# Values projected token-major, and their convolution by shifted reads of a scratch

## The chip, the cores and the metric

One core of a Trainium2 chip runs the whole layer. The metric is the device time of one execution in microseconds; the time of a kernel is the median of its runs. The engines are TensorE (PE, with its weight loads as PEld), VectorE (DVE), ScalarE (ACT), GpSimd (POOL) and SyncE (SP), which issues nearly all DMAs in order.

## The reference

A decoder layer with two parallel mixers over 256 tokens of width 2048, everything in float32. Cut to what matters here:

```python
h = rms_norm(x, norm_pre_w) * (1 + scale) + shift
proj = h @ w_in                                   # 24656 columns
qkv = causal_conv_silu(gdn_qkv, gdn_conv_w)       # 4 taps over tokens, each channel by itself
q_a, k_a, v_a = split(qkv)                        # 16 heads of q and k, 32 of v, 128 channels each
q_a, k_a = l2_normalize(q_a) * 128**-0.5, l2_normalize(k_a)   # each serves two value heads
o_a = gated_delta_rule(q_a, k_a, v_a, g_log, beta)            # a unit lower triangular solve
o_a = rms_norm(o_a, gdn_norm_w) * silu(gdn_z)
y_a = o_a @ w_proj_gdn
# mLSTM branch y_b (its own conv of q and k), then
out = (sigmoid(gate_a) * y_a + sigmoid(gate_b) * y_b) @ w_out
return x + gate * rms_norm(out, norm_post_w)

def causal_conv_silu(x, w):
    xp = pad(x, 3 tokens in front)
    return silu(sum(xp[:, j:j + s] * w[j] for j in range(4)))
```

## The kernel before

All large products run on TensorE as three matmuls for each float32 product. A weight piece (`raw`, 128x1024 of a 1 MB load) is split by ScalarE into a high part (`whi`, L173) and by VectorE into the rest (`wlo`, L177); `h` is held split as `h_hi` and `h_lo`.

`Stream` walks one list of weight pieces in order. It loads ahead into three 1 MB buffers, prepares (splits) up to four pieces ahead of use into four buffers of each part, emits the matmuls of a piece, and then calls `side.step()` once. Everything that is not a weight product is written as a generator in `Side`: at each step every generator runs to its next `yield`, so a `yield from wait(3)` means that three weight pieces go by. `side.debt` counts VectorE microseconds, 1.6 are forgiven a step, and `side.room` holds the triangular solve back while the debt is high. The whole order on each engine is fixed when the program is built; on the chip an engine waits in order for what it needs. A tile's next use in its ring of buffers waits for the readers of its last.

A weight group has 512 columns, and two forms of product:

- `add_proj_t` (`pt`, L639 and L643): channels on partitions, tokens on the free axis. The weights are the stationary operand; a 512-column matmul moves `h_hi` and `h_lo` together and a 256-column one moves `h_hi` against the low weights. The group goes in two halves of 256 columns, four pieces each.
- `add_proj_n` (`pn`, through `mm3`, L244): tokens on partitions. `h` is stationary and 512 weight columns move, three matmuls for each block of 128 tokens and of the depth. Eight pieces.

A GDN period `gdn_period(zg)` covers two head pairs, `2 * zg` and `2 * zg + 1`. A head pair is one group of 512 columns: q, k and two value heads. The stream has the first pair (8 pieces, `add_proj_t`), the z group (8, `add_proj_n`) and the second pair (8). There are eight periods, and then four mLSTM periods, the two output projections and the last product.

For a head pair `conv_half` does the convolution channel-major, where a token shift is a shift on the free axis: q and k as the first half, the two values as the second. It adds the two parts of the projection (L688), scales by the last tap (ScalarE, L691), adds the other three taps with six VectorE instructions (L697) and takes the silu (L705). `gdn_stage1` then splits q and k (L752), loads the decay rows (`gb`, L723), masks them on GpSimd (`dd`, L730), makes the products of k with k and q (`psa`, `psb`), transposes k (L766) and the two values (`psv`, L771), takes the exponentials (L738 to L740) and writes the scaled score matrices `au`. The values go out of `psv` scaled by the norm of k into `rr` (L812). `block_rows` writes diagonal blocks to a DRAM scratch `ud`, `base_inverse` reads them back as `ug` (L832) and solves on VectorE (L838 to L857), and `gdn_stage2`, 31 steps after the first stage, applies the inverse to `rr`.

`gates` runs once before, ahead of the GDN stage, and makes the decay rows. `late_c["gcv"]` holds the conv weights with channels on partitions.

Of the kernel before, what the change touches and what calls it, by code (L numbers as in the profile page):

```python
# [15 lines left out]
P = 128  # L16
# [102 lines left out]
def hybrid_layer_kernel(  # L119
# [41 lines left out]
    def load_w(src):  # L161
        raw = wp.tile([P, 2048], F32, name="raw", tag="raw", bufs=3)
        c = 0
        for s_ in src if isinstance(src, tuple) else (src,):
# [108 lines left out]
    gate_row_dr = dr.tile([1, D], F32, name="gate_row_dr")  # L273
    START = [40 + g for g in range(8)] + [33, 37, 34, 38, 35, 39]
# [260 lines left out]
    def gates(ps):  # L535
# [52 lines left out]
        SP.dma_start(rows[32:40], mm_[64:72])  # L588
        yield from wait(3)
# [6 lines left out]
        V.tensor_scalar(ngt, tt[:, :, 0:32], -1.0, None, op0=ALU.mult)  # L596

# [28 lines left out]
    def add_proj_t(g, first, after, extra=None):  # L626

        w = w_in[g].rearrange("p (k n) -> p k n", k=KC)
        st_ = {}
        for hf in range(2):  # L630
            for t in range(2):
# [20 lines left out]
                stream.add(w[:, t * 8:(t + 1) * 8, hf * S:(hf + 1) * S], prep_w, use, after=done if t else None)  # L652
# [3 lines left out]
    def add_proj_n(g, after, extra=None):  # L656

        st_ = {}
        for t in range(4):
            def use(h, hi, lo, t=t):  # L660
                if t == 0 and h == 0:
                    st_["ps"] = [jtile(f"pn{i}") for i in range(2)]
                for kc in range(2):
                    k = t * 4 + h * 2 + kc
                    o = kc * 512
                    for b in range(2):
                        mm3(st_["ps"][b], h_hi[:, k, b * P:(b + 1) * P], h_lo[:, k, b * P:(b + 1) * P],
                            hi[:, o:o + 512], lo[:, o:o + 512], k == 0, k == KC - 1)
            stream.add(w_in[g][:, t * 2048:(t + 1) * 2048], prep_w, use, after=
                       (lambda: after(st_["ps"])) if t == 3 else None)  # L670
            if extra:
                extra()

    def conv_half(ps, taps, dst, hf, add=1, late=0, home=0, whole=False):

        if home and hf == 0:
            pair = bp.tile([P, 2, S], F32, name="ab", tag="ys", bufs=1)
            ab = [pair[:, i] for i in range(2)]
        elif home:
            ab = [bp.tile([P, S], F32, name="ab", tag=t, bufs=1) for t in ("p2", "tmp")]  # L680
        else:
            ab = [yp.tile([P, S], F32, name="ab", tag=("ya", ("yhi", "ylo")[i])[hf], bufs=3 - hf) for i in range(2)]
# [23 lines left out]

    def gdn_qk(ps, taps, qs, r, late):

        yield from conv_half(ps, taps, qs, 0, 1, late)
        qh = bp.tile([P, 2, S], F32R, name="qh", tag="qh", bufs=1)  # L710
        A.copy(qh, qs[:, 0:2])
        r.update(qh=qh)
# [29 lines left out]
    def gdn_taps(p):  # L742
        return lambda n, j: late_c["gcv"][:, (p * 4 + n) * 4 + j:(p * 4 + n) * 4 + j + 1]

    def gdn_stage1(p, ps, qs, pr, res):
# [6 lines left out]
        V.tensor_tensor(ql, qs[:, 0:2], qh.bitcast(F32), op=ALU.subtract)  # L752
        yield
        gb = decay_rows(2 * p)
# [4 lines left out]
        yield from banks(3)  # L759
# [5 lines left out]
        for m in range(2):  # L765
            T.transpose(psb[:, 256 + m * P:256 + (m + 1) * P], qs[:, 0, m * P:(m + 1) * P], ident)  # L766
        psv = gtile("psv", True)
        side.debt -= 1.6
        for blk in range(2):
            for h in range(2):  # L770
                T.transpose(psv[:, (blk * 2 + h) * P:(blk * 2 + h + 1) * P],  # L771
                            qs[:, 2 + h, blk * P:(blk + 1) * P], ident)
# [6 lines left out]
        if z == 0:  # L779
            res["eq"] = bp.tile([P, 2, 2], F32, name="eq", tag="eq", bufs=3)  # L780
            res["rr"] = bp.tile([P, 2, 2, S], F32, name="rr", tag="rr")
# [13 lines left out]
        for blk, ps_, n, c0 in ((0, psa, 256, 0), (1, psb, 128, 512)):  # L795
# [8 lines left out]
            if blk == 0:  # L804
                sk = bp.tile([P, 2], F32, name="sk", tag="sk")
# [3 lines left out]
        block_rows(res, z)  # L809
        yield  # L810
        for blk in range(2):
            A.activation(res["rr"][:, blk, z], psv[:, blk * S:(blk + 1) * S], AF.Copy, scale=sk[:, blk:blk + 1])  # L812
        gfree(psv)
# [66 lines left out]
    def gdn_stage2(zg, res, zr):  # L880
# [71 lines left out]

        rr = res["rr"].rearrange("p b z (h d) -> p b (z h d)", h=2)
# [81 lines left out]
    def period_tail(zg, ps, qs, pr, res, zr):  # L1035
        yield from gdn_stage1(2 * zg + 1, ps, qs, pr, res)
# [14 lines left out]
    def gdn_period(zg):  # L1051
        res = {}

        def pair(z, after):
            p, pr = 2 * zg + z, {}
            add_proj_t(p, lambda ps, qs: gdn_qk(ps, gdn_taps(p), qs, pr, 2 if z else 5),
                       lambda ps, qs: side.add(after(ps, qs, pr)))
# [499 lines left out]
```

## Time and profile before

| | |
|---|---|
| median of 3 runs | 1570.53 us (1570.4 to 1570.74) |
| profiled execution, its own time | 1570.67 us |
| its span | 1568.9 us |
| granted TensorE clock, mean | 0.998 |
| GDN stage, one period | 79.0 us, 24 weight pieces |
| GDN stage in the trace | about 334 to 966 us |
| mLSTM stage | to about 1180 us |

The span is cut into stages by time; a window of 79 us inside the GDN stage holds one period's work of every kind, though of three different periods, since the solve and the second stage trail the projection. Busy time of matmuls counts overlapping ones more than once, so the time of a matmul in a stream is read from one start to the next. A row such as `L697 DVE ... x24 | 10.1, 477 | 0.0` gives line, engine, operation, tiles, shapes and count, then busy us, mean ns of one, and the idle time before them with what ended it.

### The profile page before, as it was taken

The page shows a single profiled execution, that of the slowest core. Times are in us where ns is not written, and L with a number is a line of the kernel's source. Part 1 is how long each engine was busy: PE and PEld are TensorE (multiplying, and loading weights), DVE is VectorE, ACT ScalarE, POOL GpSimd, SP SyncE. Part 2 cuts the span into 40 slices and gives each one's busy share as a digit, 9 for nine tenths or more (in the row PEclk, how much of TensorE's full clock was granted, in tenths as well). Part 3 has the DMA queues.
Part 4 walks back from the last instruction along what each step waited for, and adds up shares of the span by engine and source line. Part 5 has one row for each costly group of instructions (what it writes and reads, how often), then busy time and mean ns, then how long its engine had stood idle before and what let it go on. Part 6 is the DMA issues. An engine that isn't in the chain of part 4 may idle for free.

```text
span 1568.9 us, 23204 instructions
## 1 busy us (share of the span) xinstructions
PE 1555.8 (99%) x8574; PEld 1308.5 (83%) x8574; DVE 1166.0 (74%) x1901; ACT 967.5 (62%) x1629; POOL 261.5 (17%) x212
## 2 busy tenths in 40 slices
PE   8999999999999999999999999999999999999997
PEld 5888888888888888888888888888888888888886
DVE  6785556765789898989898988776868866756654
ACT  7754446765666676767676777766566554544443
POOL 5787771000000010101010101000000000100100
PEclk9999999999999999999999999999999999999999
DMA  9998775975565656565656565657779877766573
GB/s 379 403 387 328 274 282 196 287 251 194 171 209 174 194 166 201 172 200 173 200 173 200 173 200 179 194 166 250 274 271 343 312 268 290 287 237 243 211 268 108
DMA packets 167739, 372.22 MB, mean 237 GB/s; under 512 B 26021, under 2 KB 127797, under 8 KB 140105
## 3 DMA queue, kind: packets, MB, share of 16 engines
q1 hardware_dynamic: 167240, 370.13, 68.2%
q8 instruction: 67, 1.10, 0.3%
q10 hardware_dynamic: 290, 0.53, 0.1%
q14 instruction: 46, 0.38, 0.1%
q0 software_dynamic: 96, 0.09, 0.0%
HBM read 354.40 MB, written 16.31 MB: 236 GB/s over the span
## 4 chain that ended last, share of the span: by engine, by line
PE 83%; issue 13%; DMA 2%; POOL 1%; ACT 1%; DVE 0%; SPq 0%; DVEq 0%; POOLq 0%; ACTq 0%
PE pn L244 38%; PE pt L639 19%; PE pt L643 9%; PE py L244 8%; POOL mg L1347 1%; DMA raw<-in_dram 1%; PE psa L244 1%; PE csil L314 0%; PE po L989 0%; PE po L988 0%; PE pc L978 0%; PE pb L968 0%; PE pa L960 0%; PE po L986 0%; PE pt L1028 0%
## 5 line engine op out<-in xcount | busy, mean ns | idle before, releaser
L177 DVE TENSOR_TENSOR wlo<-raw,whi 128x1024 fp32r<-128x1024 f32 (+1 forms) x455 | 558.8, 1236 | 221.6 <-ACT whi L173 220.5
L173 ACT CAST whi<-raw 128x1024 fp32r<-128x1024 f32 x508 | 523.9, 1046 | 269.4 <-PE pn L244 138.0
L244 PE MATMUL pn<-whi,h 128*128 128x512 f32 x1792 | 563.8, 392 | 1.2 <-ACT part L488 0.5
L639 PE MATMUL pt<-h,whi 128*128 128x512 f32 x1280 | 407.9, 400 | 0.0
L244 PEld LDWEIGHTS pn<-whi,h 128*128 128x128 f32 x1792 | 336.3, 188 | 72.3 <-ACT h L173 1.1
L244 PE MATMUL pn<-wlo,h 128*128 128x512 f32 x896 | 348.8, 389 | 0.0
L643 PEld LDWEIGHTS pt<-h,wlo 128*128 128x128 f32 x1280 | 240.4, 188 | 56.6
L643 PE MATMUL pt<-h,wlo 128*128 128x256 f32 x1280 | 251.9, 278 | 0.0
L639 PEld LDWEIGHTS pt<-h,whi 128*128 128x128 f32 x1280 | 195.5, 189 | 1.9
L244 PEld LDWEIGHTS pn<-wlo,h 128*128 128x128 f32 x896 | 168.3, 188 | 33.6
L177 POOL TENSOR_TENSOR wlo<-raw,whi 128x1024 fp32r<-128x1024 f32 (+1 forms) x67 | 146.5, 2199 | 47.3 <-ACT whi L173 41.6
L244 PE MATMUL py<-whi,yhi 128*128 128x512 f32 x384 | 150.6, 392 | 0.0
L244 PE MATMUL py<-whi,ylo 128*128 128x512 f32 x384 | 149.6, 390 | 0.0
L244 PE MATMUL py<-wlo,yhi 128*128 128x512 f32 x384 | 149.4, 389 | 0.0
L173 ACT CAST yhi<-ya 128x512 fp32r<-128x512 f32 x48 | 29.9, 623 | 127.6 <-PE py L244 124.3
L486 DVE TENSOR_TENSOR part<-pn,part 128x512 f32<-128x512 f32 x112 | 73.8, 686 | 45.1 <-PE pn L244 44.9
L730 POOL TENSOR_SCALAR_AFFINE_SELECT dd<-gb 128x256 f32<-128x256 f32 x40 | 33.9, 870 | 435.4 <-DMA gb<-rows 398.9
L177 DVE TENSOR_TENSOR ylo<-ya,yhi 128x512 fp32r<-128x512 f32 x48 | 33.2, 691 | 75.3 <-ACT yhi L173 71.8
L244 PEld LDWEIGHTS py<-whi,yhi 128*128 128x128 f32 x384 | 72.1, 188 | 15.3
L244 PEld LDWEIGHTS py<-whi,ylo 128*128 128x128 f32 x384 | 72.1, 188 | 15.1
L244 PEld LDWEIGHTS py<-wlo,yhi 128*128 128x128 f32 x384 | 72.1, 188 | 14.9
L697 DVE SCALAR_TENSOR_TENSOR qs<-ab,gcv,qs 128x255 f32<-128x255 f32 (+2 forms) x192 | 81.0, 477 | 0.0
(264 smaller groups left out, 1602.8 us busy)
## 6 DMA issues: line engine op xcount, KB each, us to landing
raw<-in_dram SPq DMA_DIRECT2D x259, 1024.0 KB
ar<-in_dram SPq DMA_DIRECT2D x31, 1024.0 KB
raw<-in_dram SPq DMA_DIRECT2D x16, 512.0 KB
ya<-o_dr SPq DMA_DIRECT2D x32, 256.0 KB
gate_dr<-part SPq DMA_DIRECT2D x11, 512.0 KB
gb<-rows SPq DMA_DIRECT2D x20, 256.0 KB
raw<-in_dram SPq DMA_DIRECT2D x6, 768.0 KB
ug<-ud SPq DMA_DIRECT2D x32, 128.0 KB
```

Of the source, the lines that this page charges most:

```text
L173: A.copy(hi, src)
L177: eng.tensor_tensor(lo, src, hi.bitcast(F32), op=ALU.subtract)
L244: T.matmul(ps, l, r, start=start and i == 0, stop=stop and i == 2, skip_group_check=True)
L486: V.tensor_tensor(part[g][:, b], ps[b], part[g][:, b], op=ALU.add)
L639: T.matmul(ps, hi[:, o:o + P], h2[:, k].rearrange("p a s -> p (a s)"), start=k == 0, stop=k == KC - 1, skip_group_check=True)
L643: T.matmul(ps[:, 0:S], lo[:, o:o + P], h_hi[:, k], start=False, stop=k == KC - 1, skip_group_check=True)
L697: V.scalar_tensor_tensor(dst[:, n, sh:], ab[i][:, 0:S - sh], taps(n, 3 - sh), dst[:, n, sh:], op0=ALU.mult, op1=ALU.add)
L730: G.affine_select(dd[:, :, blk * S:blk * S + P], gb[:, :, blk * P:(blk + 1) * P], pattern=[[0, 2], [1, P]], compare_op=ALU.is_ge, fill=-1e ...
L1347: G.tensor_tensor(mcols(b, hf, cg), mcols(b, hf, cg), s_, op=ALU.add)
```

## The change

The q and k halves of both head pairs of a period now form one channel-major group (two halves of 256 columns, one for each pair, 8 pieces); the four value heads form one token-major group of 512 columns (`add_proj_n`, 8 pieces); z follows. The weight arrays stay as they are: the two groups are read as column halves of the two old ones, so a unit of value weights is loaded with two DMAs.

The values are copied out of PSUM into `rr`, tokens on partitions. A token shift is now a shift across partitions, so they are written to a DRAM scratch `vd` with three zero rows in front, and read back shifted by one, two and three tokens. The tap weights are needed along the free axis: they are transposed once in `gates`, written to a scratch `conv_dr`, and read broadcast to all partitions, `ws`, for each pair. For each pair GpSimd multiplies shifts 2 and 3 by their taps and adds them, VectorE does so for shifts 0 and 1, and VectorE adds the two sums. One silu covers all four heads, and four ScalarE instructions scale by the norm of k. The transposes `psv` and the separate `gdn_qk` are gone. `conv_half` keeps its q and k work, now inside `gdn_stage1`, with its temporary in the ring `ylo`.

```diff
     def load_w(src):
...
+        for i, s_ in enumerate(src if isinstance(src, tuple) else (src,)):
+            if isinstance(src, tuple) and len(s_.shape) == 3:
+                SP.dma_start(raw.rearrange("p (k g c) -> p k g c", k=4, g=2)[:, :, i], s_)
+                continue
...
+    conv_dr = dr.tile([NPAIR, 4, 4, P], F32, name="conv_dr")
+    vd = dr.tile([S + 3, 512], F32, name="vd")
...
 # in gates
+        for z in range(2):
+            SP.dma_start(vd[0:3, z * S:(z + 1) * S], zz[0:3])
...
+        G.tensor_copy(gcp.rearrange("c (p t n) -> c p t n", n=4, t=4),
+                      late_c["gcv"].rearrange("c (p n t) -> c p t n", n=4, t=4))
+        yield from wait(2)
+        tc_ = gtile("tc")
+        for b in range(2):
+            T.transpose(tc_[:, b * P:(b + 1) * P], gcp[:, b * P:(b + 1) * P], ident)
+        A.copy(gct, tc_[:, 0:S])
+        yield from wait(2)
+        for b in range(2):
+            SP.dma_start(conv_dr[8 * b:8 * b + 8].rearrange("p t n c -> (p t n) c"), gct[:, b * P:(b + 1) * P])
...
 # in gdn_stage1
-        yield from conv_half(ps, gdn_taps(p), qs, 1, *((1, 0) if z else (3, 1)))
-        qh = pr["qh"]
+        yield from conv_half(ps, gdn_taps(p // 2), qs, z)
+        qz = qs[:, 2 * z:2 * z + 2]
+        qh = bp.tile([P, 2, S], F32R, name="qh", tag="qh", bufs=1)
+        A.copy(qh, qz)
+        gb = decay_rows(2 * p)
+        yield from wait(1 + z)
...
-        yield from banks(3)
+        yield from banks(2)
...
-        psv = gtile("psv", True)
-        side.debt -= 1.6
-        for blk in range(2):
-            for h in range(2):
-                T.transpose(psv[:, (blk * 2 + h) * P:(blk * 2 + h + 1) * P],
-                            qs[:, 2 + h, blk * P:(blk + 1) * P], ident)
+        side.debt -= 1.2
...
-        for blk in range(2):
-            A.activation(res["rr"][:, blk, z], psv[:, blk * S:(blk + 1) * S], AF.Copy, scale=sk[:, blk:blk + 1])
-        gfree(psv)
+    def gdn_values(zg, ps, res):
+        rr = bp.tile([P, 2, 2, S], F32, name="rr", tag="rr")
+        for b in range(2):
+            A.copy(rr[:, b].rearrange("p z c -> p (z c)"), ps[b])
+        yield from wait(2)
+        SP.dma_start(vd[3:].rearrange("(b t) c -> t b c", b=2), rr.rearrange("p b z c -> p b (z c)"))
+        ws = [bp.tile([P, 4, S], F32, name="cw", tag="qs") for _ in range(2)]
+        def tap_rows(z):
+            SP.dma_start(ws[z], conv_dr[2 * zg + z, :, 2:4].rearrange("t n c -> t (n c)").unsqueeze(0)
+                         .broadcast_to([P, 4, S]))
+        def shifted(z, j):
+            v = yp.tile([P, 2, S], F32, name=f"v{j}", tag="yhi" if z and j > 1 else "ya", bufs=2 if z and j > 1 else 3)
+            SP.dma_start(v, vd[3 - j:3 - j + S, z * S:(z + 1) * S].rearrange("(b t) c -> t b c", b=2))
+            return v
+        def tap(e, z, v, j):
+            side.debt += 0.7 if e is V else 0.0
+            e.tensor_tensor(v, v, ws[z][:, 3 - j].unsqueeze(1).broadcast_to([P, 2, S]), op=ALU.mult)
+        def plus(e, a, b):
+            side.debt += 0.7 if e is V else 0.0
+            e.tensor_tensor(a, a, b, op=ALU.add)
+        tap_rows(0)
+        yield from wait(3)
+        vs = [[rr[:, :, z], None, None, None] for z in range(2)]
+        for z, j in ((0, 1), (0, 2), (0, 3), (1, 2), (1, 3)):
+            vs[z][j] = shifted(z, j)
+        tap_rows(1)
+        yield from wait(3)
+        for z in range(2):
+            v = vs[z]
+            tap(G, z, v[2], 2)
+            tap(G, z, v[3], 3)
+            plus(G, v[2], v[3])
+            tap(V, z, v[0], 0)
+            yield
+            tap(V, z, v[1], 1)
+            yield
+            plus(V, v[0], v[1])
+            if z == 0:
+                vs[1][1] = shifted(1, 1)
+            yield
+            plus(V, v[0], v[2])
+            yield
+        A.activation(rr, rr, AF.Silu)
+        yield
+        for z in range(2):
+            for b in range(2):
+                A.activation(rr[:, b, z], rr[:, b, z], AF.Copy, scale=res["sk", z][:, b:b + 1])
+        res["rr"] = rr
...
 # in gdn_period
-        pair(0, lambda ps, qs, pr: gdn_stage1(2 * zg, ps, qs, pr, res))
+        pair = 2 * zg, 2 * zg + 1
+        add_proj_t(pair, lambda ps, qs: gdn_stage1(pair[0], ps, qs, res),
+                   lambda ps, qs: side.add(period_tail(zg, ps, qs, res, zrs[zg])))
+        add_proj_n(pair, lambda ps: side.add(gdn_values(zg, ps, res)))
         add_z(zg)
-        pair(1, lambda ps, qs, pr: period_tail(zg, ps, qs, pr, res, zrs[zg]))
```

More of the change, by code (lines that the diff above doesn't have):

```diff
@@ L626, in add_proj_t @@
     def add_proj_t(g, first, after, extra=None):
-        w = w_in[g].rearrange("p (k n) -> p k n", k=KC)
         st_ = {}
         for hf in range(2):
+            w = w_in[g[hf] if isinstance(g, tuple) else g].rearrange("p (k n) -> p k n", k=KC)
+            c0 = 0 if isinstance(g, tuple) else hf * S
             for t in range(2):
@@ L651, in done @@
                         after(st_["ps"], st_["dst"])
-                stream.add(w[:, t * 8:(t + 1) * 8, hf * S:(hf + 1) * S], prep_w, use, after=done if t else None)
+                stream.add(w[:, t * 8:(t + 1) * 8, c0:c0 + S], prep_w, use, after=done if t else None)
                 if extra:
@@ L668, in use @@
                             hi[:, o:o + 512], lo[:, o:o + 512], k == 0, k == KC - 1)
-            stream.add(w_in[g][:, t * 2048:(t + 1) * 2048], prep_w, use, after=
+            if isinstance(g, tuple):
+                src = tuple(w_in[i].rearrange("p (k n) -> p k n", k=KC)[:, 4 * t:4 * t + 4, S:2 * S] for i in g)
+            else:
+                src = w_in[g][:, t * 2048:(t + 1) * 2048]
+            stream.add(src, prep_w, use, after=
                        (lambda: after(st_["ps"])) if t == 3 else None)
@@ L681, in conv_half @@
         else:
-            ab = [yp.tile([P, S], F32, name="ab", tag=("ya", ("yhi", "ylo")[i])[hf], bufs=3 - hf) for i in range(2)]
+            pair = yp.tile([P, 2, S], F32, name="ab", tag="ylo", bufs=2)
+            ab = [pair[:, i] for i in range(2)]
         for i in range(2):
@@ L705, in conv_half @@
         A.activation(dst[:, 2 * hf:2 * hf + 2], dst[:, 2 * hf:2 * hf + 2], AF.Silu)
[L707 to L712, printed above, removed]
     o_dr = dr.tile([32, P, S], F32, name="o_dr")
@@ L740, in decay_exp, with gdn_taps, taps, gdn_stage1 @@
             A.activation(dd[:, h, S:384], dd[:, h, S:384], AF.Exp, bias=b22[:, h:h + 1])
-    def gdn_taps(p):
-        return lambda n, j: late_c["gcv"][:, (p * 4 + n) * 4 + j:(p * 4 + n) * 4 + j + 1]
-    def gdn_stage1(p, ps, qs, pr, res):
-        z = p % 2
-        yield from conv_half(ps, gdn_taps(p), qs, 1, *((1, 0) if z else (3, 1)))
-        qh = pr["qh"]
+    def gdn_taps(zg):
+        def taps(n, j):
+            c = ((2 * zg + n // 2) * 4 + n % 2) * 4 + j
+            return late_c["gcv"][:, c:c + 1]
+        return taps
+    def gdn_stage1(p, ps, qs, res):
+        z = p % 2
+        yield from conv_half(ps, gdn_taps(p // 2), qs, z)
[4 more added lines that the diff above has]
+        yield from wait(1 + z)
         side.debt += 0.7
         ql = bp.tile([P, 2, S], F32R, name="ql", tag="ql", bufs=1)
-        V.tensor_tensor(ql, qs[:, 0:2], qh.bitcast(F32), op=ALU.subtract)
-        yield
-        gb = decay_rows(2 * p)
+        V.tensor_tensor(ql, qz, qh.bitcast(F32), op=ALU.subtract)
         dd = decay_mask(gb)
@@ L804, in gdn_stage1 @@
             if blk == 0:
-                sk = bp.tile([P, 2], F32, name="sk", tag="sk")
+                res["sk", z] = sk = bp.tile([P, 2], F32, name="sk", tag="sk", bufs=4)
                 pow_(sk, sse[:, 2:4], phalf[:, 0:2])
@@ L951, in gdn_stage2 @@
         yield
+        while "rr" not in res:
+            yield
         rr = res["rr"].rearrange("p b z (h d) -> p b (z h d)", h=2)
@@ L1033, in gdn_stage2, with period_tail @@
             SP.dma_start(o_dr[4 * zg + 2 * z:4 * zg + 2 * z + 2].rearrange("h d t -> d h t"), oT)
-    def period_tail(zg, ps, qs, pr, res, zr):
-        yield from gdn_stage1(2 * zg + 1, ps, qs, pr, res)
+    def period_tail(zg, ps, qs, res, zr):
+        yield from gdn_stage1(2 * zg + 1, ps, qs, res)
         yield
@@ L1052, in gdn_period @@
         res = {}
[L1054 to L1057, printed above, removed]
-        pair(0, lambda ps, qs, pr: gdn_stage1(2 * zg, ps, qs, pr, res))
+        pair = 2 * zg, 2 * zg + 1
+        add_proj_t(pair, lambda ps, qs: gdn_stage1(pair[0], ps, qs, res),
+                   lambda ps, qs: side.add(period_tail(zg, ps, qs, res, zrs[zg])))
+        add_proj_n(pair, lambda ps: side.add(gdn_values(zg, ps, res)))
         add_z(zg)
-        pair(1, lambda ps, qs, pr: period_tail(zg, ps, qs, pr, res, zrs[zg]))
     def mlstm_taps(m):
```

5 lines of the change are left out of this document (2 added, 3 removed).

## The prediction

> **What bounds the kernel now.** I read the busy table first, then the windows of single stages, then the chain that ended last and TensorE's own list of waits.
>
> ```profile
> span 1568.9 us, 23204 instructions
> PE 1555.8 (99%) x8574; PEld 1308.5 (83%) x8574; DVE 1166.0 (74%) x1901; ACT 967.5 (62%) x1629; POOL 261.5 (17%) x212
> ...
> PE 83%; issue 13%; DMA 2%; POOL 1%; ACT 1%; DVE 0%; SPq 0%; DVEq 0%; POOLq 0%; ACTq 0%
> ```
>
> ```profile
> core 0: us, PE busy (x) PEld busy (x) DVE busy (x) ACT busy (x) POOL busy (x), PEclk, DMA share, GB/s
> 0.00:334.00 334.00, 328.85 (x1443) 266.23 (x1444) 223.71 (x265) 202.67 (x267) 174.57 (x110) 1.00 0.84 313
> ...
> 571.00:650.00 79.00, 79.00 (x546) 68.33 (x545) 68.95 (x150) 56.77 (x115) 7.66 (x9) 1.00 0.59 185
> 650.00:729.00 79.00, 79.00 (x546) 68.33 (x546) 69.08 (x149) 56.77 (x115) 7.66 (x9) 1.00 0.60 185
> ```
>
> One 79 us window is one period of the GDN stage (two head pairs and a z group, 24 weight pieces, so 79 / 24 = 3.29 us a step). There are eight periods. In them TensorE is busy 79.00 of 79.00 us at full granted clock, VectorE 69.08, ScalarE 56.77. TensorE's waits in the whole program come to 5.3 us, none of them in this stage:
>
> ```profile
> PE csil L314 <- ACT ar L312: 4.0, 1, 4.0
> PE pn L244 <- ACT part L488: 0.5, 1, 0.5
> PE pn L244 <- DVE part L490: 0.5, 1, 0.5
> PE pn L244 <- ACT h L173: 0.3, 1, 0.3
> ```
>
> So the period lasts as long as TensorE's instruction list takes to issue. A change here is worth what it removes from that list, unless it makes a feeder late.
>
> **TensorE, the term that counts.** A busy row double-counts pipelined matmuls, so I take start-to-start times from the timeline:
>
> ```profile
> 640.20 0.63 PE L639 MATMUL pt<-h,whi 128*128 128x512 f32 x2
> 640.66 0.40 PE L643 MATMUL pt<-h,wlo 128*128 128x256 f32 x2
> ...
> 651.34 0.62 PE L639 MATMUL pt<-h,whi 128*128 128x512 f32 x2
> ...
> 653.31 0.60 PE L771 MATMUL psv<-con,qs 128*128 128x128 f32 x4
> 653.66 0.48 PE L244 MATMUL pn<-whi,h 128*128 128x512 f32 x1
> ...
> 656.29 0.61 PE L244 MATMUL pn<-whi,h 128*128 128x512 f32 x2
> ...
> 661.73 0.61 PE L244 MATMUL pn<-whi,h 128*128 128x512 f32 x2
> ```
>
> 1. Channel-major (pt): 16 rounds of two 512- and two 256-column matmuls from 640.20 to 651.34, 0.696 us each. Token-major (pn): 8 rounds of three 512-column matmuls from 656.29 to 661.73, 0.680 us. Both rounds stream 1536 columns and a piece has four, so a piece costs 2.785 against 2.72 us. The first pn rounds after an insertion are slower (653.66 to 656.29 is 2.63 us for 11 matmuls, 0.717 a round), 0.14 us over 11 x 0.227 and so about 0.02 on each of the group's eight pieces: an estimate of 2.74. The change turns 8 pieces a period, 64 in all, from pt to pn: 64 x 0.045 to 0.065 = 2.9 to 4.2 us. I take 3.5, the middle, since v's group will also have insertions in it.
> 2. The transposes psv of the values go, since the values arrive token-major: 653.31 to 653.66, 0.35 us for four, once in each of 16 first stages: 5.6 us.
> 3. Added: two transposes of the conv weights in the gate stage, at under 0.1 us each by the psv row, plus the switch of shape: 0.3 us.
>
> Sum: 1570.67 (profiled execution: span 1568.9 and 1.8 around it) - 3.5 - 5.6 + 0.3 = 1561.9 us. That execution lies 0.14 us over the median of the runs, which is nothing here. Order and width of the rest of TensorE's list do not change.
>
> **VectorE.** It has 9.9 us free in a period; the change must not spend them.
>
> ```profile
> L177 DVE TENSOR_TENSOR wlo<-raw,whi 128x1024 fp32r<-128x1024 f32 x24 | 29.3, 1220 | 7.4 <-ACT whi L173 7.4
> L697 DVE SCALAR_TENSOR_TENSOR qs<-ab,gcv,qs 128x255 f32<-128x255 f32 (+2 forms) x24 | 10.1, 477 | 0.0
> ...
> L688 DVE TENSOR_TENSOR ab<-pt,ab 128x256 f32<-128x256 f32 x8 | 3.0, 416 | 0.0
> ...
> L752 DVE TENSOR_TENSOR ql<-qs,qh 128x512 fp32r<-128x512 f32 x2 | 1.4, 685 | 0.0
> ```
>
> The values' half of the convolution goes: 12 of 24 at L697 (5.05 us) and 4 of 8 at L688 (1.5). Added are, for each head pair, two tap products and two sums of 128x512 from SBUF, 8 a period, priced by L752 at 0.685: 5.5 us. Net -1.05: about 68.0 of 77.9 us. Slack is as before.
>
> **GpSimd**, six 128x512 instructions a period (two products and a sum for each pair). Its nearest rows are the merges near the end, which meet VectorE's weight splits:
>
> ```profile
> L1347 POOL TENSOR_TENSOR mg<-mg,gs x8: 1285/2046/2295, 1343.0 to 1477.1; 128x512 f32<-128x512 f32 x8
> ```
>
> ```profile
> 1343.28 2.07 DVE L177 TENSOR_TENSOR wlo<-raw,whi 128x1024 fp32r<-128x1024 f32 x1
> ...
> 1347.07 4.53 DVE L177 TENSOR_TENSOR wlo<-raw,whi 128x1024 fp32r<-128x1024 f32 x2
> ```
>
> Alone 1.285 us, in company 2.0: 7.7 to 12.3 us a period on an engine with 7.66 busy, and each sum is first read three steps (9.9 us) after its chain of three was issued; hidden. But VectorE pays too: its splits there took 2.07 instead of 1.22 and 4.53 instead of 2.44, 2.9 us lost to four GpSimd instructions, 0.73 each. Six cost 4.4 us a period; bounds 0 (no overlap) and 6 x 1.285 = 7.7. VectorE comes to 72.4 of 77.9 us, at worst 75.7: still below TensorE. What covers it locally is the lead of the split weights over TensorE, which is least behind ScalarE's exponentials:
>
> ```profile
> 649.26 1.05 ACT L173 CAST whi<-raw 128x1024 fp32r<-128x1024 f32 x1 [1.78 <-PE pt L639]
> 650.33 1.28 ACT L738 ACT_TABLE_LOAD   x1
> 653.30 0.40 ACT L738 ACTIVATE dd<-dd,ngt 128x128 f32<-128x128 f32 x1 [1.69 <-POOL dd L730]
> ...
> 656.46 2.02 ACT L173 CAST whi<-raw 128x1024 fp32r<-128x1024 f32 x2
> ```
>
> ```profile
> 657.56 1.23 DVE L177 TENSOR_TENSOR wlo<-raw,whi 128x1024 fp32r<-128x1024 f32 x1 [2.47 <-ACT whi L173]
> ```
>
> The pn pieces start at 653.66, about 656.5, 659.2 and 661.96. With four buffers the cast of 656.46 is for the fourth: its low half is ready at 658.79, 3.2 us before use. One burst of three GpSimd instructions costs VectorE 2.2 us by the measured loss: covered. The Trainium skill (SBUF — State Buffer, Who interferes with whom) says that a VectorE instruction with two SBUF inputs and a GpSimd instruction that reads SBUF exclude each other for the whole instruction. The two L177 rows agree in kind; in a fully exclusive reading each GpSimd instruction would cost VectorE its whole length, which leaves the sum at 1561.9 as long as the lead holds and else gives the lock rival below.
>
> **ScalarE**, from its groups in the same window:
>
> ```profile
> L691 ACT ACTIVATE qs<-ab,gcv 128x256 f32<-128x256 f32 x8 | 3.6, 508 | 0.0
> L684 ACT COPY ab<-pt 128x256 f32<-128x256 f32 x8 | 2.6, 377 | 0.0
> ...
> L705 ACT ACTIVATE qs<-qs 128x512 f32<-128x512 f32 x4 | 2.5, 633 | 1.0 <-DVE qs L697 1.0
> ...
> L812 ACT ACTIVATE rr<-psv,sk 128x256 f32<-128x256 f32 x4 | 1.7, 470 | 0.0
> L1047 ACT ACTIVATE sz<-pn 128x512 f32<-128x512 f32 x2 | 1.1, 588 | 0.0
> ```
>
> Gone: half of L691, L684 and L705 (4.35) and the psv reads (1.7). Added: two 128x512 copies out of PSUM (1.1), one silu of 1024 (about 1.05, by the cast of that size), four scalings (1.7). Net -2.2: nothing, under TensorE. By the counts of waits in the code the two first stages now lie 5 steps apart, where a z group stood between them, so the exponentials (650.33 to 655.3) come twice in quick succession, with three or four casts to recover between them.
>
> **DMA and SP.** A period gains a 0.52 MB write, six shifted reads of 0.26 MB and two tap broadcasts of 0.52 MB: 3.1 MB on 14.6 (185 GB/s x 79 us), 228 GB/s in 77.9 us; the first stage runs at 313. SP issues 13 DMAs more (9 of these, 4 for the split value weights). At 2.70 / 4 = 0.68 us that is 9 us of an SP that mostly waits for buffers. The shifted reads wait on SP for the write to land, with the weight loads queued behind them; the write has three steps (9.9 us) by then, and the bound is a scratch of this kernel:
>
> ```profile
> SPq L864 <- DMA xd<-xx: 34.5, 7, 5.0
> ```
>
> 34.5 / 7 = 4.9 us at a small size, so the wait is short or nothing. VectorE needs its first shifted copy four steps (13.2 us) after the issue. The nearest row is the read of the other scratch:
>
> ```profile
> 673.08 2.70 SPq L832 DMA_DIRECT2D ug<-ud  x4
> ```
>
> ```profile
> 684.93 0.17 DVE L840 TENSOR_SCALAR nsu<-ug 128x15 f32<-128x15 f32 x1 [0.69 <-DMA ug<-ud]
> ```
>
> It took 11.9 us, in a busy stretch of the queues, and VectorE waited 0.69 us without TensorE feeling it. The shifted copies fit by 1.3 us, and the lead of 3.2 stands behind that. ug itself is now issued a step behind 1.8 MB of these reads, 5.7 us at 313 GB/s, so its wait may grow by as much: mostly the lead again. GpSimd waits for its copies too; only later decay masks queue behind it, which already wait for their own rows.
>
> **Rivals.**
> - *Late scratch reads.* VectorE is in order; the weight splits stand behind its tap products. TensorE starves once a copy lands later than 13.2 + 3.2 = 16.4 us after issue. At 17.5 us it loses 1.1 us a period, 8.8 in all: 1570.7. For it: ug's 11.9. Against it: each read is small and the mean DMA share is 0.60.
> - *The lock, slower.* GpSimd excludes VectorE for whole instructions: the two bursts of three, four steps apart, cost 7.7 us. The lead takes 3.2, VectorE's free time (9.9 / 24 = 0.41 a step) 1.6 in four steps; 2.9 us a period are left, 23 in all: 1585. It decides from a stall of 1.1 us a period, that is from 5.9 us, 0.98 an instruction. Against it: 0.73 measured, and the bursts lie some eight steps from the exponentials, where the lead is longer.
> - *ScalarE's crowd.* The second exponentials find the lead not rebuilt: half a microsecond a period, 1566.
> - *No difference between pn and pt* leaves 5.3 us: 1565.3, inside my own range.
>
> **How the numbers follow.** Forecast 0.60 (own range 1559.5 to 1565.5), late reads 0.16, lock 0.12, crowd 0.10, still better than the forecast 0.02. A measurement here tells 0.2%, 3.1 us, so faster is under 1567.4 and slower over 1573.7. Faster: 0.60 + 0.02 + 0.08 of the crowd + 0.02 of the late reads = 0.72. Same: 0.11 of the late reads and 0.02 of the crowd, 0.13. Slower: the lock and 0.03 of the late reads, 0.15. The range 1559.5 to 1572 leaves out the lock, the late reads beyond 1572 (0.03) and the better case: 0.17.
>
> **What would show it.** Right: period windows of about 77.9 us with TensorE busy throughout, no psv rows, pn rows for v at 0.68 us a round, VectorE at 68 to 73 us. Late reads: VectorE idle on DMA at the tap products, and TensorE waiting for wlo. Lock: two-input VectorE rows stretched by GpSimd's tap products, and TensorE gaps there. The prediction is wrong if TensorE's waits in the stage exceed a few microseconds, whoever causes them.

## The result and the profile after

The changed kernel takes 1621.15 us (median; 1619.24 to 1622.14) against 1570.74 us before: a ratio of 1.0317, 95% interval 1.0302 to 1.0332. The forecast was 1561.9 us with 1572 as its upper end. It is 59 us too low, and the sign is wrong.

From the page of the changed kernel, the span, the busy engines and the chain that ended last:

```profile
span 1619.4 us, 22630 instructions
...
PE 1558.5 (96%) x8256; PEld 1300.2 (80%) x8256; DVE 1174.4 (73%) x1837; ACT 952.2 (59%) x1574; POOL 339.7 (21%) x261
...
PE 59%; issue 14%; DMA 12%; DVE 9%; ACT 3%; SPq 2%; POOL 1%; DVEq 0%; POOLq 0%; ACTq 0%
```

Before, TensorE held 83% of that chain and DMA 2%. Now DMA holds 12% and VectorE 9%. GpSimd is busy 78 us more and every other engine within 16 us of before, none but TensorE near the span, so the loss is waiting. The waits of the changed kernel by engine and line (us in total, times, the longest) give the places:

```profile
PE mp L968 <- DVE ycmp L935: 38.5, 4, 11.3
PE pa L1029 <- ACT x L1015: 7.7, 3, 3.0
...
DVE nsu L907 <- DMA ug<-ud: 63.8, 8, 16.2
ACT whi L176 <- DMA raw<-in_dram: 78.0, 22, 10.6
```
```profile
SPq L931 <- DMA xd<-xx: 45.1, 7, 6.9
```

TensorE stands 46.2 us in seven gaps, one in each full period: 9 to 11.3 us at `mp` in one period, 2.1 to 3.0 us at `pa` in the next. The second stage of the GDN heads waits there for the triangular solve. Before, TensorE had no wait in this stage.

One of the four long gaps, in order of time. First SP's queue, then VectorE, then TensorE (start, length, what was waited for in brackets):

```profile
470.84 2.79 SPq L843 DMA_DIRECT2D v<-vd  x5
473.73 0.41 SPq L838 DMA_DIRECT2D cw<-conv_dr  x1
474.27 1.05 SPq L927 DMA_DIRECT2D xd<-xx  x1
482.42 3.10 SPq L931 DMA_DIRECT2D xcmp<-xd  x4
485.56 2.57 SPq L899 DMA_DIRECT2D ug<-ud  x4
```
```profile
478.31 0.68 DVE L852 TENSOR_TENSOR rr<-rr,v 128x512 f32<-128x512 f32 x1
...
495.19 0.17 DVE L907 TENSOR_SCALAR nsu<-ug 128x15 f32<-128x15 f32 x1 [16.20 <-DMA ug<-ud]
...
498.00 0.44 DVE L935 STREAM_TRANSPOSE ycmp<-xcmp 128x256 f32<-128x256 f32 x1
```
```profile
486.92 0.39 PE L662 MATMUL pt<-h,wlo 128*128 128x256 f32 x2
498.58 0.65 PE L968 MATMUL mp<-ycmp,au 32*32 32x32 f32 x32 [11.27 <-DVE ycmp L935]
```

Five shifted reads of the scratch and a tap row stand on SP just ahead of `xd`, the solve's result. `xd` is issued at 474.27 and lands 8.1 us later, behind them. SP waits for it, because its next instruction is the gather of `xcmp`, and only then, at 485.56, can it issue `ug` for the next period. VectorE has reached `nsu`, which reads `ug`, and stands 16.2 us on it. `ycmp`, which TensorE needs, is behind `nsu` in VectorE's order. Three queues in order, each standing on the one before it.

The same stop holds the weights. ScalarE's rows in this gap:

```profile
478.76 1.05 ACT L176 CAST whi<-raw 128x1024 fp32r<-128x1024 f32 x1 [1.73 <-PE pt L658]
498.06 1.04 ACT L176 CAST whi<-raw 128x1024 fp32r<-128x1024 f32 x1 [10.59 <-DMA raw<-in_dram]
```

The weights for the second cast were issued on SP at 488.24, behind `ug`. With four buffers and 2.79 us a piece, the piece cast at 478.76 is the one due when TensorE stops at 487.2. So `ug` in time would have moved this gap by one piece, some 3 us, and not closed it: an estimate from these rows, which no run tests by itself.

The transfer queues are not full on average but they are in the stretch that counts. Slices of 10 us of the changed kernel (TensorE, its loads, VectorE, ScalarE, GpSimd busy; granted clock, DMA share, GB/s):

```profile
630.00:640.00 10.00, 10.00 (x50) 8.38 (x49) 9.83 (x21) 5.26 (x7) 0.70 (x1) 1.00 0.96 304
640.00:650.00 10.00, 10.00 (x50) 8.41 (x49) 6.03 (x7) 6.45 (x9) 0.00 (x0) 1.00 0.97 305
650.00:660.00 10.00, 10.00 (x59) 8.71 (x59) 5.93 (x4) 3.62 (x6) 9.38 (x6) 1.00 0.34 89
660.00:670.00 10.00, 1.24 (x8) 0.90 (x6) 3.00 (x10) 0.33 (x1) 0.00 (x0) 0.73 0.95 250
...
680.00:690.00 10.00, 10.00 (x65) 8.48 (x65) 8.96 (x21) 7.65 (x15) 0.00 (x0) 1.00 0.42 123
```

The scratch's write and reads fall in 630 to 650. At 650 the queues run a third full while SP stands on `xd`. At 660 `ug` and two late weight loads fill them again, and TensorE does 1.24 us of work in ten.

The kernel before already had such a stretch, the one in which its `ug` was issued at 673.08:

```profile
670.00:680.00 10.00, 10.00 (x91) 8.06 (x95) 7.00 (x13) 9.77 (x19) 0.00 (x0) 1.00 0.93 294
680.00:690.00 10.00, 10.00 (x125) 8.58 (x126) 8.01 (x25) 6.40 (x12) 0.00 (x0) 1.00 0.91 235
```

A long gap then costs more than its length. Two windows right after the 11.3 us gap, and two after the 3.0 us one:

```profile
498.58:502.58 4.00, 4.00 (x42) 3.45 (x43) 3.82 (x9) 3.92 (x9) 0.00 (x0) 0.50 0.92 300
502.58:506.58 4.00, 4.00 (x64) 3.34 (x64) 3.84 (x11) 1.61 (x7) 0.00 (x0) 0.81 0.81 253
```
```profile
584.70:587.70 3.00, 2.96 (x15) 2.63 (x16) 2.86 (x8) 2.53 (x6) 0.00 (x0) 0.72 1.01 334
587.70:590.70 3.00, 3.00 (x15) 2.63 (x14) 2.93 (x8) 1.18 (x2) 0.00 (x0) 0.71 0.34 105
```

After each of the four long gaps the granted clock stays at 0.50 for 4.6 to 5.7 us. After the 3.0 us gap it is 1.00 for 1.2 us and then 0.52 from 585.9 to 589.3, which the two windows show as 0.72 and 0.71. After the gaps of 2.1 and 2.5 us it stays at 1.00. In windows of 2 us over the stage the lowered clock costs 12.5 us of TensorE's work, 10.8 of them behind the four long gaps. The Trainium skill (TensorE: Matmul & The Clock Gate, Part 1) gives a free-running window of about 3.4 us, after one idle window of which the clock is halved until one busy window has passed. The trace agrees for the long gaps. The 3.0 us gap is shorter than that window and still 3.4 us near half clock follow it, and so they do after a gap of 2.35 us in kernel 11 below: there the measurement goes beyond the page.

### The profile page after: what moved, and what is told of

It is laid out like the page before. It is cut to its first block, busy times and chain, and to the rows that moved or that the text cites. A ratio compares the mean times of both kernels' runs of the same rounds, so it can differ in the third digit from the quotient of the medians.

```text
span 1619.4 us, 22630 instructions
## 1 busy us (share of the span) xinstructions
PE 1558.5 (96%) x8256; PEld 1300.2 (80%) x8256; DVE 1174.4 (73%) x1837; ACT 952.2 (59%) x1574; POOL 339.7 (21%) x261
## 3 DMA queue, kind: packets, MB, share of 16 engines
q8 instruction: 65, 1.06, 0.3%
## 4 chain that ended last, share of the span: by engine, by line
PE 59%; issue 14%; DMA 12%; DVE 9%; ACT 3%; SPq 2%; POOL 1%; DVEq 0%; POOLq 0%; ACTq 0%
PE pn L247 36%; PE py L247 8%; PE pt L658 7%; DVE wlo L180 3%; PE pt L662 3%; DMA xd<-xx 3%; DMA raw<-in_dram 3%; DMA ug<-ud 3%; SPq L931 1%; ACT whi L176 1%; DVE xx L922 1%; POOL mg L1414 1%; DMA v<-vd 1%; DVE tmp L918 1%; DVE au L816 1%
## 5 line engine op out<-in xcount | busy, mean ns | idle before, releaser
L247 PE MATMUL pn<-whi,h 128*128 128x512 f32 x2304 | 731.5, 393 | 1.4 <-ACT part L493 0.7
L180 DVE TENSOR_TENSOR wlo<-raw,whi 128x1024 fp32r<-128x1024 f32 (+1 forms) x455 | 566.9, 1255 | 204.0 <-ACT whi L176 202.5
L247 PEld LDWEIGHTS pn<-whi,h 128*128 128x128 f32 x2304 | 432.7, 188 | 91.2 <-ACT part L493 1.2
L247 PE MATMUL pn<-wlo,h 128*128 128x512 f32 x1152 | 449.1, 390 | 0.1
L658 PE MATMUL pt<-h,whi 128*128 128x512 f32 x768 | 252.9, 411 | 0.0
L247 PEld LDWEIGHTS pn<-wlo,h 128*128 128x128 f32 x1152 | 216.6, 188 | 42.9 <-POOL wlo L180 0.6
L662 PEld LDWEIGHTS pt<-h,wlo 128*128 128x128 f32 x768 | 149.0, 194 | 36.3 <-DVE wlo L180 0.8
L662 PE MATMUL pt<-h,wlo 128*128 128x256 f32 x768 | 155.3, 284 | 0.0
L658 PEld LDWEIGHTS pt<-h,whi 128*128 128x128 f32 x768 | 122.2, 195 | 2.2
L247 PE MATMUL pw<-whi,m 128*128 128x512 f32 x256 | 80.2, 391 | 0.0
```

The costliest lines, as they stand in the source:

```text
L180: eng.tensor_tensor(lo, src, hi.bitcast(F32), op=ALU.subtract)
L247: T.matmul(ps, l, r, start=start and i == 0, stop=stop and i == 2, skip_group_check=True)
L658: T.matmul(ps, hi[:, o:o + P], h2[:, k].rearrange("p a s -> p (a s)"), start=k == 0, stop=k == KC - 1, skip_group_check=True)
L662: T.matmul(ps[:, 0:S], lo[:, o:o + P], h_hi[:, k], start=False, stop=k == KC - 1, skip_group_check=True)
```

## The experiments

Theory A was that the scratch's transfers push the solve's chain back; theory B that the solve's end now meets the next `ug` on SP, whatever the scratch does. Rival C was the lock of VectorE by GpSimd, from the prediction. Kernels 1, 4, 7, 11 and 13 leave out part of the computation, to price it; the others compute all of it. All times are medians and each ratio is to the kernel before on the same chip, with its 95% interval. Steps are counted in the code from the issue of `ug`; a period has 24.

**1. Without the scratch.**

```diff
-        SP.dma_start(vd[3:].rearrange(...), rr.rearrange(...))
-            SP.dma_start(v, vd[3 - j:3 - j + S, z * S:(z + 1) * S].rearrange(...))
-            e.tensor_tensor(v, v, ws[z][:, 3 - j]..., op=ALU.mult)
+            e.tensor_tensor(v, ws[z][:, 3 - j]... if j else v, ws[z][:, 3 - j]..., op=ALU.mult)
```

> The scratch of the values is neither written nor read; the shifted taps multiply the tap row by itself, so the engines' instructions stay and 2.1 MB of DMA a period and their place in SP's queue go (the tap broadcasts stay). Theory A (the shifted reads stand in front of the solve's two scratches, SP waits in order, ug and the weights come late, VectorE waits for ug and TensorE for ycmp): the time falls to 1560 to 1568 us, the forecast of the changed list. Theory B (the two first stages now follow so closely that one period's xd and the next one's ug meet in the queue, whatever the values do): over 1600 us, ug waits of 6 us or more stay. Theory C (GpSimd's lock on VectorE): about 1621 us, since GpSimd's instructions stay.

1591.0 us, 1.0126 (1.0111 to 1.0141). Between the two theories: 30 us go, 20 stay, and the gaps at `mp` shrink from 9 to 11.3 us to about 5. Its waits:

```profile
PE mp L966 <- DVE ycmp L933: 20.3, 4, 5.5
```
```profile
SPq L929 <- DMA xd<-xx: 41.9, 7, 7.0
```

SP still stands 6 us on each `xd`, with no scratch in the way. In this kernel the taps read nothing of the scratch either, so the 30 us are its transfers and any wait for them together.

**2. The gather of xcmp later**, so that SP issues `ug` and weights instead of standing.

```diff
-        yield from wait(2 * (zg // 7))
+        yield from wait(3 - (zg // 7))
         xcmp = bp.tile([P, 8, 32], F32, name="xcmp", tag="xcmp", bufs=1)
...
-        yield from wait(5 - 2 * (zg // 7))
+        yield from wait(3)
```

> The reads xcmp<-xd are issued three steps after the write xd instead of in the same step, and waited for three steps instead of five: the same bytes, but SP no longer stands still until xd has landed (6.5 to 8.1 us in the profile after). Theory A in its form 'SP's wait': ug and the weights go out some 8 us earlier, VectorE's waits for ug fall from 63.8 to under 30 us in all, time 1585 to 1600 us. Theory A in its form 'bytes in front of ug': ug still lands late behind 1.8 MB of reads, time 1605 to 1620 us. Theory C: 1621 us.

1600.67 us, 1.0189 (1.0174 to 1.0205): 20.5 us go, just short of what the form "SP's wait" allowed. SP's wait for `xd` falls to 5.3 us, VectorE's for `ug` from 63.8 to 28.9. The edit also puts `ycmp` six steps after `xd` instead of five, so that a little of the gain may be hidden.

**3. The shifted reads four steps later**, and with them the taps, which follow the reads by three steps.

```diff
         tap_rows(0)
-        yield from wait(3)
+        yield from wait(7)
```

> The shifted reads and the second tap broadcast are issued four steps later, after ug instead of before xd and ug; nothing is left out. Theory A: ug lands with nothing of the values in front, its waits fall below 15 us in all, and the time to 1562 to 1575 us. Theory of plain DMA volume (25 MB more than the queues can hide): the same bytes, so over 1605 us. Theory B: over 1600 us. Theory C: 1621 us.

1650.32 us, 1.0498 (1.0481 to 1.0516). Worse. Theory A missed: VectorE still waits 54.1 us for `ug`, which it had below 15, and SP still stands 38.9 us on `xd`. The time is within the bounds of the others, over 1600 and 1605, though none of them expected a loss. The reads now stand behind `ug` with the weights queued after them. ScalarE's wait for weights rises from 78 to 101.9 us, and TensorE waits 18.6 us at `mp`, 15.0 at `mq` and in many smaller places.

**4. Without GpSimd's taps.**

```diff
-            tap(G, z, v[2], 2)
-            tap(G, z, v[3], 3)
-            plus(G, v[2], v[3])
```

> GpSimd's two products and its sum are left out for each head pair, the values' second half is added as read. All DMAs stay. Theory C: VectorE loses nothing to GpSimd, 1585 us or less. Theory A: within 5 us of 1621, since VectorE still stands at ug and at the shifted copies.

1621.93 us, 1.0322 (1.0306 to 1.0337): no difference to the changed kernel. VectorE is busy 22.1 us less (1152.3 against 1174.4) and waits 19.1 us more for `ug` (82.9 against 63.8). The lock decides nothing here. (It does later.)

**5. A planner step of 1.8 us**, which brings `xd` to step 20 in every period, away from `ug`. Theory B gets its sharper form here: it is the meeting of `xd` with `ug` that costs.

```diff
-STEP_US = 1.6
+STEP_US = 1.8
```

> One constant changes: 1.8 us of VectorE debt are forgiven a step instead of 1.6. The solve's last write xd then falls 20 steps after its ug in every period; in the kernel after it falls 24 and 20 steps in turn, 24 being the step at which the next period issues its ug, and before the change 19. Nothing is left out and no byte moves. Theory B, sharpened (where the solve ends in the step of the next ug, SP stands at xd's landing with ug and the weights behind it, and VectorE stands at ug ahead of the transpose ycmp that TensorE waits for): the four gaps of 9 to 11 us at mp go and leave the 2 to 3 us ones of the other periods, time 1578 to 1592 us. Theory A alone (the shifted reads in front of ug): they stay one step ahead of ug, so over 1610 us.

1628.01 us, 1.0363 (1.0347 to 1.0379). Theory B missed. Step 20 is where the next write of the scratch and its tap row are issued: `xd` met those instead. SP issues them at 545.37 and 546.00, `xd` at 546.92, and stands until 554.55; the shifted reads and `ug` go out after that. TensorE waits at `pa` now, 34.1 us in six gaps.

**6. The taps not counted as debt**, so the solve ends at step 15. **7. The same without the scratch. 8. The same as 6 with the write one step and the reads two steps earlier.**

```diff
         def tap(e, z, v, j):
-            side.debt += 0.7 if e is V else 0.0
...
         def plus(e, a, b):
-            side.debt += 0.7 if e is V else 0.0
```

> VectorE's tap products and sums are no longer counted as debt; the instructions are the same. The solve writes xd 15 steps after ug, nine steps before the next ug and eight before the shifted reads. Theory B: TensorE's gaps nearly all go, 1561 to 1575 us, what is left being ug behind the shifted reads. Theory A alone: over 1605 us. If instead VectorE is now too full where the solve runs (no pacing against the taps), TensorE waits for wlo rather than for ycmp, 1575 to 1600 us.

> As the kernel without the debt of the taps, and the values' scratch neither written nor read (the shifted taps multiply the tap row by itself). Theory B with A as its smaller part: 1559 to 1564 us, TensorE's list with no gap; the difference to the same kernel with its scratch is the price of the shifted reads, 0 to 12 us. If pacing is the limit, it is as slow as that one.

> As the kernel without the debt of the taps, and the write of the scratch is issued one step and its reads two steps earlier, three steps ahead of ug; the taps stay in their steps. Nothing is left out. Theory A as the smaller part: ug no longer queues behind the reads and the time is 1560 to 1568 us, at or below the kernel without the debt. If the reads do not matter once the solve ends in time, both are the same within 2 us.

1616.56 us (1.029, 1.0271 to 1.0309), 1583.66 (1.0078, 1.0061 to 1.0095) and 1606.08 (1.0224, 1.0206 to 1.0242). The scratch costs 33 us in this pacing as it cost 30 in the other. Taking the solve's end away from `ug` brings 4.6 us, where theory B expected over 46; the reads two steps earlier bring 10 more, where at least 48 were expected, and VectorE's wait for `ug` halves from 44.0 to 20.7 us. But this pacing has a cost of its own, so that the 4.6 us are no price of the meeting. Kernel 7 has no scratch and is still some 20 us over its expected 1564, with TensorE standing on VectorE: 8.0 us at `psa`, 5.3 at `pc`, 3.3 at `pn`.

**9 and 10. The values' group third in a period instead of second**: their write then stands 4 steps and their reads 7 steps after `ug`, in the stretch where the queues were a third to a half full. The second tap row is loaded after the first pair's taps, and `au` has four buffers to make room. Kernel 9 does not count the taps, kernel 10 counts them with a step of 1.8 us.

```diff
-        add_proj_n(pair, lambda ps: side.add(gdn_values(zg, ps, res)))
         add_z(zg)
+        add_proj_n(pair, lambda ps: side.add(gdn_values(zg, ps, res)))
...
-        tap_rows(1)
         yield from wait(3)
...
                 vs[1][1] = shifted(1, 1)
+                tap_rows(1)
...
+            if z == 0:
+                yield from wait(2)
```

> The groups of a period run in the order q and k, z, values, so the write of the value scratch stands 4 steps after the broadcast of ug and its shifted reads 7 steps after, where the transfer queues were a third to a half busy; the second tap row is loaded after the first head pair's taps into one buffer, and au has four buffers instead of five; the taps don't count in the pacing, so the store of xd stands 15 steps after ug, 9 ahead of the next. Theory A (the scratch's traffic costs by the stretch in which it stands, and the solve's end by meeting ug): both meetings are gone, the wait of VectorE for ug falls below 15 us in all, no wait of TensorE over 2 us in a full period, 1562 to 1585 us, what is left being VectorE ahead of psa and pc. Theory B (the scratch's traffic costs by its volume, wherever it stands): some 30 us stay, as between the kernels with and without it in both pacings, 1605 to 1620 us.

> The same order of groups, with the taps counted in the pacing as in the changed kernel and the planner's step set to 1.8 us instead of 1.6, so that xd stands 16 to 23 steps after ug, 16 in most periods. Theory A: as the kernel without the count, 1562 to 1585 us, and less VectorE ahead of psa and pc, since the pacing holds the solve back where the taps are. Theory B: 1605 to 1625 us.

1627.12 us (1.0357, 1.0341 to 1.0372) and 1633.11 (1.0399, 1.0382 to 1.0417; the median of three runs, as a fourth took 6739 us). Both theories missed the time, but the profile of 9 shows a new reason: in this stage VectorE stands on no transfer for over 2.2 us, and it is full. Its waits, and two windows of 30 us:

```profile
PE psa L247 <- DVE ql L777: 25.9, 7, 4.2
PE pn L247 <- DVE wlo L180: 12.6, 16, 3.2
DVE nsu L908 <- DMA ug<-ud: 5.9, 5, 2.2
```
```profile
660.00:690.00 30.00, 30.00 (x203) 26.27 (x202) 28.85 (x62) 15.55 (x33) 4.08 (x3) 1.00 0.64 222
690.00:720.00 30.00, 23.82 (x95) 18.32 (x94) 29.30 (x52) 20.98 (x46) 12.56 (x11) 0.89 0.56 167
```

VectorE is busy 58.15 of 60 us: the queries' and keys' convolution, the solve, the weight splits and now the taps. The place that is free for the queues is the place that is full for VectorE.

**11. No scratch and the gather later**: edits 1 and 2 together, in the order and pacing of the changed kernel.

> The scratch is neither written nor read (the shifted products take the tap rows alone), and the gather of xcmp is issued three steps after xd's store, so that SP stands before neither: both causes named so far are out while the order and the pacing of the changed kernel stay. Theory A (scratch traffic, and SP standing on xd ahead of ug): the waits at mp fall from 5 us to under 1.5 us, 1562 to 1575 us. Theory B (xd's and ug's meeting in one step costs by itself, whoever stands on what): gaps at mp of 3 us and more stay, 1582 to 1592 us.

1572.46 us, 1.0011 (1.0001 to 1.002). The two edits bring 30 and 20.5 us alone and 48.7 together: the two causes add up, and are nearly all of the loss against the kernel before. Some 11 us over the forecast stay. TensorE still waits 8.6 us at `mp`, up to 2.4 at a time, where theory A expected under 1.5.

**12. Kernel 9 with the taps eight steps later**, at steps 18 to 26, where VectorE had room. The transfers stay where they are.

```diff
             vs[z][j] = shifted(z, j)
-        yield from wait(3)
+        yield from wait(11)
```

> As the kernel with the values' group third in a period and the taps not counted (1627 us, without a wait of TensorE or of VectorE for a transfer of the scratch or of ug over 2 us, and VectorE 9.8 of 10 us busy for 55 us of each period), with the taps begun 8 steps later, 18 to 26 steps after ug, where VectorE was 3.5 to 7.8 of 10 us busy; the scratch's transfers stay where they are. Theory A (there the taps alone cost, by crowding VectorE ahead of psa, pn's wlo and the next solve): the 4.2 us at psa in each period fall below 2 us and the time to 1575 to 1600 us. Theory B (the scratch's traffic costs by its volume, through the loads of weights, whose wlo then comes late): 1615 to 1630 us.

1572.74 us, 1.0009 (0.9999 to 1.0019): just below theory A's range. The whole computation, all of its traffic, and 48 us of the changed kernel's loss gone by order and pacing alone.

**13. Kernel 12 without GpSimd's part** (edit 4). **14 and 15. Kernel 12 with the taps two steps later and two earlier** (`wait(13)`, `wait(9)`).

> The kernel with the values' group third and the taps 8 steps later (1572.7 us), with GpSimd's two products and its sum left out of both head pairs; VectorE's part stays. Theory A (what keeps that kernel some 9 us above the forecast's sum is GpSimd's price on VectorE, now that no transfer is waited for: where both work, VectorE's tap took 1.77 us instead of 0.68 and two wlo 2.31 and 3.77 instead of 1.22 and 2.44, about 3.5 us a period in a stretch that is full): no wait at psa over 0.3 us, 1562 to 1567 us. Theory B (VectorE's own taps crowd it, GpSimd costs nothing): 1570 to 1574 us.

> The whole computation, the values' group third, the taps begun 10 steps later instead of 8. Theory A: GpSimd's first four products then run behind psa's reads instead of ahead of them, so the 0.8 us at psa go, while those at the next pn or at mp may stay: 1566 to 1572 us. Theory B: what the taps cost by their number moves with them, 1571 to 1577 us; the last product of the solve goes out one step later than with 8, which costs nothing by itself.

> The whole computation, the values' group third, the taps begun 6 steps later instead of 8, the other way on the same line: they stand deeper in the stretch where VectorE was 9.8 of 10 us busy. Theory A and Theory B alike: slower than with 8, 1575 to 1600 us; at the same time as with 8 the fullness of VectorE would not be what decides between 1627 and 1573 us.

1560.67 us (0.9938, 0.9925 to 0.9951), 1578.31 (1.0042, 1.0028 to 1.0055) and 1598.44 (1.0183, 1.0167 to 1.0199). GpSimd's part costs 12.1 us here. Earlier, TensorE waits 17.3 us at `psa`; later, it waits 5.8 us at `pa` for the values themselves, which neither theory of 14 had. The same stretch with GpSimd (kernel 12) and without (kernel 13), VectorE's rows:

```profile
613.24 1.78 DVE L848 TENSOR_TENSOR rr<-rr,cw 128x512 f32<-128x512 f32 x1
614.93 2.31 DVE L180 TENSOR_TENSOR wlo<-raw,whi 128x1024 fp32r<-128x1024 f32 x1
...
626.70 3.76 DVE L180 TENSOR_TENSOR wlo<-raw,whi 128x1024 fp32r<-128x1024 f32 x2
630.39 1.77 DVE L848 TENSOR_TENSOR rr<-rr,cw 128x512 f32<-128x512 f32 x1
```
```profile
620.54 2.35 DVE L180 TENSOR_TENSOR wlo<-raw,whi 128x1024 fp32r<-128x1024 f32 x2
622.81 0.68 DVE L848 TENSOR_TENSOR rr<-rr,cw 128x512 f32<-128x512 f32 x1
```

Two taps of 1.77 instead of 0.68, one split of 2.31 instead of 1.22, two of 3.76 instead of 2.35: some 4.7 us a period. Over the program VectorE is busy 1191.2 us instead of 1154.8, which is 4.6 for each of the eight periods. How this becomes 12.1 us of TensorE's time is shown only in part: its waits at `psa` and `pn`, 3.5 and 3.0 us in kernel 12, are gone but for 0.2, and its busy time is 6.0 us shorter (1551.1 against 1545.1) at the same clock, which no run takes apart.

**16 and 17. All taps on VectorE**, begun 8 and 9 steps later than in kernel 9.

```diff
-            tap(G, z, v[2], 2)
-            tap(G, z, v[3], 3)
-            plus(G, v[2], v[3])
+            tap(V, z, v[2], 2)
+            tap(V, z, v[3], 3)
+            plus(V, v[2], v[3])
```

> The whole computation, the values' group third, the taps 8 steps later, GpSimd's two products and its sum given to VectorE in the same steps. Theory A (GpSimd's six instructions a period cost VectorE some 3.5 us, and also come late): VectorE gets 6 x 0.68 = 4.1 us more work and none of that loss, half of it in a stretch that had room (6.3 of 10 us busy without GpSimd), so 1563 to 1571 us, below the kernel before. Theory B (what decides is that VectorE is full, and GpSimd takes at least some work off it): 1573 to 1582 us, above the same kernel with GpSimd.

> As the kernel with all taps on VectorE, begun 9 steps later instead of 8, so that fewer of the first head pair's products stand ahead of psa's reads. Theory A: 1562 to 1571 us, the better or the worse by under 3 us. Theory B: 1572 to 1582 us.

1563.76 us (0.9953, 0.9941 to 0.9966) and 1561.31 us (0.9939, 0.9925 to 0.9952): as theory A expected, the second a little below its range. With GpSimd's six instructions a period added to its own, VectorE is busy 1182.9 us in kernel 17, less than the 1191.2 of kernel 12. Kernel 17 does the whole computation and beats the kernel before by 0.6%. From its page, a window of about one period, and two slices of 10 us:

```profile
PE 1545.7 (99%) x8256; PEld 1290.8 (83%) x8256; DVE 1182.9 (76%) x1885; ACT 954.5 (61%) x1574; POOL 264.4 (17%) x213
```
```profile
650.00:727.77 77.77, 77.77 (x507) 66.34 (x507) 70.27 (x144) 54.41 (x106) 6.45 (x9) 1.00 0.73 227
```
```profile
700.00:710.00 10.00, 10.00 (x80) 8.41 (x80) 8.61 (x11) 5.55 (x10) 0.00 (x0) 1.00 0.95 268
710.00:720.00 10.00, 10.00 (x125) 8.47 (x124) 5.58 (x18) 6.52 (x11) 0.00 (x0) 1.00 1.02 279
```

TensorE is busy for all 77.77 us of the window, at full clock, with 227 GB/s in the queues (185 before, 228 forecast) and 20 us of them at a share of 0.95 to 1.02. A full queue harms nobody as long as nobody needs what stands in it.

## Why the prediction was wrong, step by step

- **TensorE's sum was right.** 1561.9 us was forecast from 3.5, 5.6 and 0.3 us; kernel 17 takes 1561.31, and its period is 77.65 us (from `pb` at 650.76 to `pb` at 728.41) against the 77.9 forecast. It has the same TensorE instructions in another order; the three terms were not measured one by one. In the changed kernel the same 8256 matmuls are busy 1558.5 us instead of 1545.7. Of these 12.8 us the windows put 12.5 on the slowed clock, a cost that the prediction had in no term. With the 46.2 us of gaps this makes 59.0 of the 59.5 us between the two spans.
- **The step that failed is the one on DMA and SP.** It priced the new traffic against means, a share of 0.60 over the period, and the traffic came in one stretch of some 20 us at 0.94 to 1.06 (kernel 6 shows 1.04 over 30 us). It called SP an engine "that mostly waits for buffers", and took `xd`'s wait, 4.9 us, only as a bound on the landing of the scratch's own write. On that write it was right: SP's list of waits has none for it. But it left the wait for `xd` at its old size and did not ask what stands behind it. That wait was 6.4 us on average, with 8.1 from issue to landing in the gap shown, and `ug` and a weight load stood behind it. And it wrote of `ug` that its wait "may grow by as much: mostly the lead again". It allowed 5.7 us, with a lead of 3.2 behind that; the longest wait grew from 1.2 to 16.2 us, since `ug` was held up on SP, not only in the queues.
- **One thing was not traced at all:** the taps' debt moves the solve. By the code, `xd` went from step 19 to steps 24 and 20 in turn, 24 being the step in which the next `ug` is issued. Kernel 2 prices SP's standing on `xd`, in whichever step, at 20.5 us, kernel 1 the scratch at 30, kernel 11 both at 48.7. How much of the 20.5 is due to the shift of `xd` is open: kernels 5 and 6 shift it, and each brings a cost of its own.
- **The late-reads rival named the right resource and the wrong victim.** VectorE never waited on its own shifted copies in the changed kernel (GpSimd did, 133.3 us in all, but VectorE's list has no wait for GpSimd's products); what was late were the transfers issued behind them.
- **The lock: the size was near, the cover was not.** 4.4 us a period were forecast; VectorE's busy time gives 2.8 in the changed kernel (22.1 us less in kernel 4, over eight periods) and 4.6 in kernel 12. It cost nothing in the changed kernel, where TensorE waited for transfers anyway (kernel 4), and 12.1 us once those waits were gone (kernel 13). The forecast set it against VectorE's free time as a mean, 9.9 us a period, and the lead of 3.2 us. VectorE's free time also lies in one stretch, and elsewhere it is full: 58 of 60 us in kernel 9.
- **ScalarE's crowd** did not appear: TensorE waits for a weight cast only in kernel 3, 5.0 us, where ScalarE itself waits for weights.
- The condition under which the prediction called itself wrong, waits of TensorE in the stage of more than a few us, is what happened.

Shown are the two causes and their sum, what GpSimd's part costs in kernel 12, and that order, pacing and the choice of engine recover the loss. Only argued is how the 30 us of the scratch divide between packets ahead of `xd`, ahead of `ug` and ahead of the weights: these can't be taken apart by leaving one out.

## What to carry to other kernels

Price a new transfer, and new work on a second engine, against the slices of the period in which it falls, not against a mean share: by the mean the queues were 40% free here and VectorE free for 9.9 of 79 us, and neither had room where the change put its work. For an instruction that waits on an in-order queue, list what is issued behind it and who waits for that, down to the engine that sets the end. When work is added to a planner's list, rebuild the list and see which steps have moved, the old ones too.

## What was not expected of the hardware

- A gap of TensorE of 9 to 11 us is followed by 4.6 to 5.7 us at a granted clock of 0.50, which adds 2.3 to 2.9 us to the gap. One of 3.0 us is followed by 3.4 us at 0.52, begun 1.2 us after the gap, and one of 2.35 us in kernel 11 by 3.4 us at 0.50; after gaps of 2.1 and 2.5 us the clock stayed at 1.00. So the length of a short gap alone does not decide.
- GpSimd's 128x512 products with two SBUF inputs stretched VectorE's instruction beside them by 1.1 to 1.4 us, and six a period cost some 4.6 us of it, against the 4.1 us that the same six take on VectorE itself (6 x 0.68): handing them over gained VectorE nothing. The Trainium skill (SBUF — State Buffer, Who interferes with whom) has the two exclude each other, and the rows agree.
